# Storing h, q and V as high and low parts in a hybrid attention layer

## The chip, the cores and the metric

The kernel runs on one core of one Trainium2 chip. The metric is the device time of one execution in microseconds (us); a lower number is better. Each figure for a kernel as a whole is a median over several executions. Times inside the kernel come from one execution that the hardware profiler recorded.

The engines are named as in the profile: PE is the matmul engine (PEld its weight loads, which overlap its matmuls), DVE the vector engine, ACT the scalar engine, POOL the GpSimd engine, SP the engine that here issues every DMA transfer.

## The reference

One decoder layer over 2048 tokens of width 1024, in float32. Only the part that the change touches is shown in full.

```python
h = _rmsnorm(x, attn_pre_norm[l])
qkv = h @ w_qkv[l]                      # 1024 x 3072
dq, dk, dv, sq, sk, sv = jnp.split(qkv, QKV_SPLITS, axis=-1)
# group A: 4 heads, two softmax maps of 64 per head, values of 128
diff_o = _diff_attention(dq, dk, dv, lam, rel_bias)
diff_o = _rmsnorm(diff_o, diff_subln[l]) * (1.0 - lam_init)
# group B: 8 heads of 64, z = q k / 8, no softmax:
#   a = exp(log_sigmoid(z) + sum over later keys of log_sigmoid(-z)), strictly causal
sb_o = _rmsnorm(_stick_breaking_attention(sq, sk, sv), sb_norm[l])
mix = jnp.concatenate([diff_o, sb_o], axis=-1) @ w_o[l]
x = x + _rmsnorm(mix, attn_post_norm[l])
h = _rmsnorm(x, ffn_pre_norm[l])
u = _causal_depthwise_conv(h @ w_up[l], conv_w[l], conv_b[l])
gate, val = jnp.split(u, 2, axis=-1)
y = (jax.nn.gelu(gate, approximate=True) * val) @ w_down[l]
x = x + _rmsnorm(y, ffn_post_norm[l])
```

## The kernel before

**High and low parts.** A matmul takes its operands in the type float32r, which keeps fewer bits than float32. Each float32 operand is therefore split: the high part is the value rounded to float32r (a cast), the low part the value minus the high part (a subtraction). A product is then three matmuls, high by high, high by low and low by high. The helper `split` (lines 454 to 462) makes both parts from a raw float32 piece in SBUF: the cast on DVE (line 457) or ACT (458), the subtraction on POOL (459) or DVE (461).

**Order of the work.** Nothing is issued where it is written. Every step is recorded as an operation with a cost in ns per engine that could do it, and `Plan.run` (line 180) then simulates the engines by these costs and issues each operation on the engine that is free first, the nominally earliest ready one first. All engines run their lists in order, so the costs (`c_act`, `c_dvp`, `c_scan` and others, lines 43 to 68) decide on which engine a copy lands and in which order. SP has one list for all transfers.

**Stages.** (1) `prep` makes h for 256 tokens at a time (8 token tiles): rows of x are normed, transposed on PE into PSUM tiles `t`, and leave PSUM three times: high part to `hT` on ACT (line 575), low part to `hT` on DVE (577), and a raw float32 copy to `ring_a` on ACT (581), from which `store_h` (588) writes h to the DRAM tensor `hd`. (2) The projection to q, k and V runs in five passes over the 8 token tiles, because only three units of 256 columns of w_qkv fit on chip at once. Pass 0 uses the `hT` that `prep` made; in passes 1 to 4 `load_h` (line 528) loads the raw h of a tile from `hd` into the ring `ring_w` and splits it into `hT`. That is 32 tiles of two halves, each half 128x1024 elements.

(3) `evac` (line 619) takes a finished product out of PSUM (`g`) through a staging tile `st` (two buffers) to DRAM. q leaves raw, scaled on ACT (line 634), and is stored by line 643 to `qd`; V leaves raw (466 or 467) and is stored by 629 to `vd`; k is already split here, high part on ACT or DVE, low part on DVE (638), both stored by 646 to `kd`.

(4) 64 attention units (g, s), g one of 8 head pairs, s one of 8 blocks of 256 queries. `load_q` (698) and `load_kv` (678) fetch their operands. k goes straight to its tile `k`. q goes raw to `ring_w` and is split into the tile `q` (two buffers); V goes raw to `ring_w` and is split into `v` (five buffers). Units with g below 4 are differential attention (`diff_front`, `diff_back`), the others stick-breaking (`sb_stream`). In a stick-breaking unit each chunk of logits goes through two sigmoids on ACT (978, 980), a running product along the keys on DVE (986, called the scan below), a multiplication on POOL (991), transposes on PE (729) to `t`, a split of these into `thi` (ACT 466 or DVE 467) and `tlo` (DVE 743), and the products with V on PE (1009). At a unit's end `fin_sb` norms the result (DVE 813, 816, 825, POOL 815). The projection's passes 1 to 4 are merged into the attention units, spread evenly.

(5) The output projection, merged with the last units, and (6) the FFN, neither of which the change touches.

The rings `ring_w` (8192 columns) and `ring_a` (4096) hold pieces of any length in order of use; the attention's rows of logits live there too.

Of the kernel before, what the change touches and what calls it, by code (L numbers as in the profile page):

```python
# [15 lines left out]
F32 = mybir.dt.float32  # L16
# [8 lines left out]
P = 128  # L25
# [16 lines left out]
# Costs in ns, by which the order of issue is planned.  # L42
# [16 lines left out]
def c_scan(n):  # L59
    return 130 + 1.6 * n  # L60
# [59 lines left out]
class Ring(Tag):  # L120
    """Pieces of any length, one after the other, round and round."""
# [145 lines left out]
def layer_kernel(  # L267
# [149 lines left out]
    def setup_bias():  # L417
# [11 lines left out]
        v4 = lambda: br.t.rearrange("p (h c) -> p h c", h=4)  # noqa: E731  # L429
# [25 lines left out]
    def split(raw, hi, lo, n, deps, bufs, lead):  # L455
        """hi + lo = raw exactly"""
# [7 lines left out]
    def copy(dst, src, n, deps, bufs, what=None):  # L464
        """out of PSUM"""
# [3 lines left out]
    class Unit:  # L469
# [55 lines left out]
    hcur, hdep, hraw, hstore, xin = {}, {}, {}, {}, {}  # L525
    qstore, kstore, vstore = defaultdict(list), defaultdict(list), defaultdict(list)

    def load_h(p, i):
        hcur[p, i] = [buf("hT"), buf("hT")]
        hdep[p, i] = []  # L530
        for c in range(2):
            h, raw = hcur[p, i][c], buf("w", 1024)
            rv = lambda raw=raw: raw.t.rearrange("p (k n) -> p k n", k=4)  # noqa: E731
            o = load(rv, hd[i][:, c * 4:(c + 1) * 4, :], 1 << 19, (raw,), (hstore[i, c],), what="hload")
            hdep[p, i] += [split(rv, lambda h=h: h.t[:, 0], lambda h=h: h.t[:, 1], 1024, (o,), (raw, h), 0.0)] * 4
# [9 lines left out]
    def prep(i, gdep):  # L545
        """x rows -> normed, transposed, split"""
# [13 lines left out]
        hraw[i] = [(buf("a", 1024), []) for _ in range(2)]  # L560
        for k2 in range(4):
# [875 lines left out]
```

## Time and profile before

| | |
|---|---|
| median of 3 runs | 3197.41 us (3193.2 to 3203.99) |
| span of the profiled execution | 3198.2 us |
| PE busy | 3010.5 us, 94% |
| PEld busy | 2627.1 us, 82% |
| DVE busy | 2370.5 us, 74% |
| ACT busy | 1550.6 us, 48% |
| POOL busy | 1141.6 us, 36% |
| DMA | 353.25 MB moved, mean 110 GB/s |

The profiled execution's span differs from the median by 0.8 us, so the span is taken as its whole time. The busy shares are means over stages that have different limits: from about 740 us on the stick-breaking heads run, from about 1460 us their end and the output projection, from about 1760 us the FFN. A row of the profile names the line, the engine, the operation, the tile written and the tiles read, the shape, the number of such instructions, and then the time.

### The profile page before, as it was taken

Reading aid. Unit: us, or ns where it says so; the run is one execution under the profiler, and the core shown is the slowest. Engines: PE = TensorE matmul, PEld = TensorE weight load, DVE = VectorE, ACT = ScalarE, POOL = GpSimd, SP = SyncE. Lnnn points to the kernel's source line nnn. Section 1 sums busy time; section 2 is a strip of 40 time slices with the busy share of each in tenths; the row PEclk is TensorE's granted clock in tenths of the full one; section 3 lists DMA queues with packets and bytes.
Section 4 is the critical chain, followed back from the end, with each engine's and each line's share of the span. In section 5 each row is a group of like instructions: output and inputs, shape, how many; then the busy total and the mean of one; then the engine's idle time right before and its main releaser. Section 6 shows DMA issues by size and latency. Waiting matters only on the chain. (4 is left out here: it accounts for less than half of the span.)

```text
span 3198.2 us, 48493 instructions
## 1 busy us (share of the span) xinstructions
PE 3010.5 (94%) x17352; PEld 2627.1 (82%) x17352; DVE 2370.5 (74%) x4310; ACT 1550.6 (48%) x3098; POOL 1141.6 (36%) x1135
## 2 busy tenths in 40 slices
PE   7999999999888788878999999999999999999998
PEld 7999999989777687777877888888888888888887
DVE  4588979898999999998865676367753877367742
ACT  5555655656666666665654343223332333223421
POOL 1131223224777777775522211023310333023310
PEclk9999999999999999998999999999999999999999
DMA  6553334423322123142245333343334433343342
GB/s 219 177 151 97 96 95 128 118 67 100 107 73 60 52 83 102 58 109 88 99 154 175 115 106 98 120 148 96 97 121 123 123 103 93 125 139 99 94 131 79
DMA packets 371669, 353.25 MB, mean 110 GB/s; under 512 B 20096, under 2 KB 311780, under 8 KB 371428
## 3 DMA queue, kind: packets, MB, share of 16 engines
q1 hardware_dynamic: 371428, 350.16, 36.3%
q8 instruction: 136, 2.23, 0.3%
q14 instruction: 105, 0.86, 0.1%
HBM read 274.58 MB, written 75.50 MB: 109 GB/s over the span
## 5 line engine op out<-in xcount | busy, mean ns | idle before, releaser
L1235 PE MATMUL pu<-fh,fhi 128*128 128x512 f32 x2816 | 868.2, 390 | 0.2 <-ACT fu L1243 0.2
L1235 PEld LDWEIGHTS pu<-fh,fhi 128*128 128x128 f32 x2816 | 529.1, 188 | 110.6 <-ACT fu L1243 0.6
L461 DVE TENSOR_TENSOR flo<-fraw,fhi 128x1024 fp32r<-128x1024 f32 x186 | 232.9, 1254 | 487.0 <-ACT fhi L458 486.9
L1235 PE MATMUL pu<-fh,flo 128*128 128x512 f32 x1408 | 548.5, 390 | 0.0
L991 POOL TENSOR_TENSOR ring_w<-ring_w,ring_a 128x512 f32<-128x512 f32 (+2 forms) x320 | 407.8, 1289 | 203.1 <-DVE ring_a L986 144.6
L458 ACT CAST fhi<-fraw 128x1024 fp32r<-128x1024 f32 x253 | 265.6, 1051 | 397.0 <-PE py L1320 220.9
L613 PE MATMUL g<-hT,big 128*128 128x256 f32 x3072 | 451.6, 288 | 3.6 <-POOL big L459 1.9
L986 DVE TENSOR_TENSOR_SCAN ring_a<-ring_a 128x513 f32<-128x513 f32 (+2 forms) x320 | 433.5, 1379 | 3.7 <-ACT ring_a L978 3.3
L1320 PE MATMUL py<-fhi,gt 128*128 128x512 f32 x1408 | 435.7, 390 | 0.0
L613 PEld LDWEIGHTS g<-hT,big 128*128 128x128 f32 x3072 | 407.3, 192 | 12.8 <-POOL big L459 2.3
L711 PE MATMUL z<-k,q 128*128 128x512 f32 (+3 forms) x1280 | 364.4, 379 | 12.6 <-ACT ring_a L978 6.1
L466 ACT CAST thi<-t 128x512 fp32r<-128x512 f32 (+2 forms) x461 | 217.8, 492 | 212.5 <-PE t L729 187.9
L459 POOL TENSOR_TENSOR flo<-fraw,fhi 128x1024 fp32r<-128x1024 f32 x78 | 195.8, 2511 | 339.2 <-DVE fhi L457 171.2
L1320 PEld LDWEIGHTS py<-fhi,gt 128*128 128x128 f32 x1408 | 264.3, 188 | 60.5
L1235 PEld LDWEIGHTS pu<-fh,flo 128*128 128x128 f32 x1408 | 264.6, 188 | 55.3
L743 DVE TENSOR_TENSOR tlo<-t,thi 128x512 fp32r<-128x512 f32 (+2 forms) x528 | 281.4, 557 | 34.0 <-ACT thi L466 25.6
L729 PE MATMUL t<-ident,ring_w 128*128 128x128 f32 x1632 | 262.3, 282 | 40.5 <-DVE tlo L743 22.1
L1259 POOL TENSOR_TENSOR gt<-fy,gt 128x512 fp32r<-128x512 f32 x88 | 118.4, 1346 | 493.9 <-ACT gt L1258 477.1
L1320 PE MATMUL py<-flo,gt 128*128 128x512 f32 x704 | 277.4, 394 | 0.0
L729 PEld LDWEIGHTS t<-ident,ring_w 128*128 128x128 f32 x1632 | 194.2, 144 | 61.5 <-issue 16.3
L1248 DVE SCALAR_TENSOR_TENSOR fy<-fu,cw,fy 128x512 f32<-128x512 f32 x176 | 239.8, 1363 | 6.2
L610 PE MATMUL g<-big,hT 128*128 128x256 f32 x1536 | 226.5, 286 | 0.0
(170 smaller groups left out, 5009.5 us busy)
## 6 DMA issues: line engine op xcount, KB each, us to landing
fraw<-in_w_up_dram SPq DMA_DIRECT2D x176, 512.0 KB, 3.8
fraw<-in_w_down_dram SPq DMA_DIRECT2D x88, 512.0 KB, 3.7
ring_w<-hd SPq DMA_DIRECT2D x64, 512.0 KB, 5.0
kd<-st SPq DMA_DIRECT2D x128, 128.0 KB, 2.5
k<-kd SPq DMA_DIRECT2D x32, 512.0 KB, 4.8
ring_w<-qd SPq DMA_DIRECT2D x128, 128.0 KB, 3.7
ring_w<-in_x_dram SPq DMA_DIRECT2D x16, 512.0 KB, 4.5
hd<-ring_a SPq DMA_DIRECT2D x16, 512.0 KB, 2.8
```

The source lines that it names most:

```text
L458: "ACT", c_act(n) + 42, lambda: nc.scalar.copy(hi(), raw()))
L461: "DVE", c_dvs(n), lambda: nc.vector.tensor_tensor(lo(), raw(), f32(hi()), ALU.subtract))
L610: nc.tensor.matmul(ps.t[:, cs], hk[:, b, c * P:(c + 1) * P], wv[:, a, k, :], start=first, stop=last)
L613: nc.tensor.matmul(ps.t[:, cs], wv[:, a, k, c * P:(c + 1) * P], hk[:, b, :], start=first, stop=last)
L711: nc.tensor.matmul(ps.t[:, 0:w], q.t[:, m, l, jj * P:(jj + 1) * P], kt.t[:, m, 0:w], start=(l == 0), stop=(l == 1 and not masked))
L729: nc.tensor.transpose(ps.t[:, cc * P:(cc + 1) * P], rows[jj].t[:, (k + kk) * P:(k + kk + 1) * P], ident)
L743: ol = op("DVE", c_dvp(n), lambda sl=sl: nc.vector.tensor_tensor(lo.t[:, sl], ps.t[:, sl], f32(hi.t[:, sl]), ALU.subtract), (oh,), (ps, hi ...
L986: nc.vector.tensor_tensor_scan(gr, gr, gr, 1.0 if cb is None else cb[0].t[:, 0:1], ALU.mult, ALU.bypass)
L991: rdeps.append(op("POOL", c_pool(w), lambda be=be, gm=gm, w=w: nc.gpsimd.tensor_tensor(be.t, be.t, gm.t[:, 1:w + 1], ALU.mult), (o1, o2), ...
L1235: nc.tensor.matmul(ps.t, w3(w)[:, k, :], h.t[:, a, k, :], start=(k == 0 and i == 0), stop=(k == KD - 1 and i == 2))
L1248: nc.vector.scalar_tensor_tensor(y.t, u.t[:, 1:TT + 1], cw[:, 1, f:f + 1], y.t, ALU.mult, ALU.add)
L1320: nc.tensor.matmul(ps.t, gt.t[:, a, j * P:(j + 1) * P], wt.t[:, ms], start=(m == 0 and i == 0), stop=(m == NFT - 1 and i == 2))
```

## The change

h, q and V are split once, where they are made, the two parts are stored side by side in DRAM, and the loads write both parts directly into the tiles that the matmuls read. `hd`, `qd` and `vd` have twice the bytes. The raw copy of h in `ring_a` and the raw pieces in `ring_w` are gone, and with them 64 splits of h, 64 of q and 32 of V. In `evac` each q and each V gets a low part on DVE (64 and 64 instructions of 128x256). The planner's cost of a scan, `c_scan`, is another one. Comments are dropped; the lines of after.py are therefore up to 9 lower.

```diff
 def c_scan(n):
-    return 130 + 1.6 * n
+    return 130 + 2.083 * n
...
-    qd = [dram.tile([64, 2, S], F32, name=f"qd{g}") for g in range(8)]
+    qd = [dram.tile([64, 2, 2, S], F32, name=f"qd{g}") for g in range(8)]
...
-    vd = [dram.tile([S, 256], F32, name=f"vd{u}") for u in range(4)]
-    hd = [dram.tile([P, KD, 256], F32, name=f"hd{i}") for i in range(8)]
+    vd = [dram.tile([2, 4, P, 4, 256], F32, name=f"vd{u}") for u in range(4)]
+    hd = [dram.tile([2, P, KD * 256], F32, name=f"hd{i}") for i in range(8)]
...
     def load_h(p, i):
...
-            h, raw = hcur[p, i][c], buf("w", 1024)
-            rv = lambda raw=raw: raw.t.rearrange("p (k n) -> p k n", k=4)
-            o = load(rv, hd[i][:, c * 4:(c + 1) * 4, :], 1 << 19, (raw,), (hstore[i, c],), what="hload")
-            hdep[p, i] += [split(rv, lambda h=h: h.t[:, 0], lambda h=h: h.t[:, 1], 1024, (o,), (raw, h), 0.0)] * 4
+            h = hcur[p, i][c]
+            o = load(lambda h=h: f32(h.t).rearrange("p a k n -> p (a k n)"), hd[i][c], 1 << 20, (h,), (hstore[i, c],),
+                     what="hload")
+            hdep[p, i] += [(o,)] * 4
...
     def prep(i, gdep):
...
-                raw, ops = hraw[i][k // 4]
-                ops.append(op("ACT", c_act(256) + 95, lambda raw=raw, pk=pk, k=k: nc.scalar.activation(
-                    raw.t[:, k % 4 * 256:(k % 4 + 1) * 256], pk(), AF.Identity, scale=g_pre[:, k:k + 1]), (o, gdep),
-                    (ps, raw)))
-        store_h(i)
...
+        for c in range(2):
+            ops = [o for pair in hdep[0, i][4 * c:4 * c + 4] for o in pair]
+            hstore[i, c] = op(SPE, 0, lambda c=c: nc.sync.dma_start(
+                hd[i][c], f32(h[c].t).rearrange("p a k n -> p (a k n)")), ops, (h[c],), 0, 1 << 20, "hstore")
...
         def evac(c):
...
             if is_v:
-                o = copy(lambda: tf()[:, 0:256], pc, 256, (st["last"],), (ps, t))
...
+                o1 = copy(lambda: t5(0), p4, 256, (st["last"],), (ps, t))
+                o = op("DVE", c_dvp(256), lambda: nc.vector.tensor_tensor(t5(1), p4(), f32(t5(0)), ALU.subtract),
+                       (o1,), (ps, t))
+                vstore[spec, i].append(op(SPE, 0, lambda: nc.sync.dma_start(
+                    vd[spec][:, r0 // 4, :, r0 % 4, :].rearrange("g p c -> p g c"),
+                    tf().rearrange("p (g c) -> p g c", g=2)), (o,), (t,), 0, 1 << 18, "vstore"))
...
             if kind == "q":
-                o = op("ACT", c_act(256), lambda: nc.scalar.activation(tf()[:, 0:256], pc(), AF.Copy, scale=0.125),
-                       (st["last"],), (ps, t))
+                o1 = op("ACT", c_act(256), lambda: nc.scalar.activation(t.t[:, 0:256], pc(), AF.Copy, scale=0.125),
+                        (st["last"],), (ps, t))
+                o = op("DVE", c_dvp(256), lambda: nc.vector.scalar_tensor_tensor(
+                    t.t[:, 256:512], pc(), 0.125, f32(t.t[:, 0:256]), ALU.mult, ALU.subtract), (o1,), (ps, t))
...
     def load_kv(g, c):
...
-        raw = buf("w", 512)
...
-            vs = split(r5, lambda: v5()[:, :, :, 0, :], lambda: v5()[:, :, :, 1, :], 512, (o,), (raw, v), 0.0)
-        kv[g, c] = (kt, v, ok, vs)
+        ov = load(lambda: f32(v.t), vd[g // 2][g % 2, c], 1 << 19, (v,),
+                  [o for i in tiles for o in vstore[g // 2, i]], what="vload")
+        kv[g, c] = (kt, v, ok, (ov,))
 
     def load_q(g, s):
-        q, raw = buf("q"), buf("w", 512)
+        q = buf("q")
...
-        qt[g, s] = q, split(rv, lambda: q.t[:, :, 0, :], lambda: q.t[:, :, 1, :], 512, ls, (raw, q), 0.0)
+        qt[g, s] = q, [load(lambda r=r: f32(q.t[r * 64:(r + 1) * 64]), qd[g][:, :, :, s * 256:(s + 1) * 256], 1 << 18,
+                            (q,), qstore[g, s], what="qload") for r in range(2)]
```

What this makes of the engines' lists is seen at two places. The first is DVE in the stick-breaking stage, at the same scans of the same unit. `hT`, `q` and `v` are matmul tiles, `ring_a` the rows of the scan, `tlo` the low part of transposed rows, `st` the staging tile of `evac`, `os`, `sq`, `sm` and `mix` tiles of `fin_sb`. Before:

```order
L743 TENSOR_TENSOR tlo_186<-t_145,thi_184 128x512
L986 SCALAR_TENSOR_TENSOR ring_a<-ring_a 128x513
L461 TENSOR_TENSOR hT_161<-ring_w,hT_161 128x1024
L816 TENSOR_REDUCE sm_204<-sq_191 128x4
L743 TENSOR_TENSOR tlo_187<-t_146,thi_185 128x512
L382 TENSOR_SCALAR sm_203<-sm_204 128x4
L986 SCALAR_TENSOR_TENSOR ring_a<-ring_a 128x513
```

And now:

```order
L734 TENSOR_TENSOR tlo_186<-t_145,thi_184 128x512
L807 TENSOR_REDUCE sm_200<-sq_191 128x4
L624 TENSOR_TENSOR st_164<-g_148,st_164 128x4x64
L382 TENSOR_SCALAR sm_205<-sm_200 128x4
L624 TENSOR_TENSOR st_165<-g_148,st_165 128x4x64
L734 TENSOR_TENSOR tlo_187<-t_146,thi_185 128x512
L977 SCALAR_TENSOR_TENSOR ring_a<-ring_a 128x513
```

The 128x1024 subtraction for `hT` out of the ring is gone from between the scans; two subtractions of 128x256 elements that read PSUM (`g`) stand there for V.

The second place is SP at the start of pass 4, with the semaphores that each transfer waits for in brackets (DMAHW is an earlier transfer). Before:

```order
L646 DMA kd_73<-st_165 64x2x256 [waits DMAHW2_49]
L377 DMA ring_w<-hd_80 128x1024 [waits DMAHW3_49]
L377 DMA ring_w<-hd_80 128x1024 [waits DMAHW4_49,Pool_49]
L775 DMA mixd_88<-mo_188 128x256 [waits DMAHW5_49,Activation_49]
L629 DMA vd_78<-st_164 128x256 [waits DMAHW6_49,Activation_49]
L629 DMA vd_78<-st_165 128x256 [waits DMAHW7_49,Activation_49]
L377 DMA ring_w<-qd_64 64x2x256 [waits DMAHW0_49,PE_49]
```

And now:

```order
L647 DMA kd_73<-st_165 64x2x256 [waits DMAHW2_49]
L766 DMA mixd_88<-mo_188 128x256 [waits DMAHW3_49,Activation_49]
L377 DMA hT_158<-hd_80 128x2048 [waits DMAHW4_49,PE_49]
L377 DMA hT_159<-hd_80 128x2048 [waits DMAHW5_49,PE_49]
L377 DMA q_179<-qd_64 64x4x256 [waits DMAHW6_49,PE_49]
L377 DMA q_179<-qd_64 64x4x256 [waits DMAHW7_49]
L626 DMA vd_78<-st_164 128x2x256 [waits DMAHW0_49,DVE_49]
```

The loads of h and q now wait for PE to release `hT` and `q` themselves, and the store of V, which waits for DVE instead of ACT, stands behind them.

## Rows read from the trace of the kernel before

**Rows 1.** The page: busy tenths in 40 slices of 80 us each.

```profile
PE   7999999999888788878999999999999999999998
DVE  4588979898999999998865676367753877367742
DMA  6553334423322123142245333343334433343342
```

**Rows 2.** Windows by stage: length, busy us (count) per engine, clock, DMA share, GB/s.

```profile
0.00:160.00 160.00, 142.55 (x1146) 138.80 (x1147) 79.12 (x222) 92.00 (x232) 23.41 (x31) 1.00 0.64 198
160.00:740.00 580.00, 560.83 (x4237) 532.36 (x4235) 508.06 (x1594) 336.51 (x706) 151.16 (x109) 0.99 0.38 107
740.00:1460.00 720.00, 597.92 (x4250) 544.69 (x4249) 693.73 (x911) 477.06 (x1061) 528.60 (x657) 0.96 0.29 83
1460.00:1760.00 300.00, 280.07 (x1438) 232.02 (x1437) 214.50 (x334) 162.66 (x403) 112.78 (x152) 0.97 0.40 130
1760.00:3198.20 1438.20, 1429.17 (x6290) 1179.21 (x6288) 875.05 (x1254) 482.39 (x697) 325.62 (x188) 1.00 0.36 112
```

**Rows 3.** Waits of PE, 740 to 1460 us: total us, times, longest.

```profile
PE t L772 <- DVE tlo L743: 34.5, 19, 3.4
PE o L1009 <- DVE tlo L743: 23.5, 26, 2.3
```

**Rows 4.** DVE by shape, 740 to 1460 us: count, busy us, mean ns, idle before.

```profile
L986 DVE TENSOR_TENSOR_SCAN ring_a<-ring_a 128x513 f32<-128x513 f32 x186 | 285.0, 1552 | 0.1
...
L825 DVE SCALAR_TENSOR_TENSOR mix<-os,sm,sbn 128x64 f32<-128x64 f32 x108 | 66.6, 675 | 1.8 <-POOL sm L384 0.9 <-POOL ring_a L976 0.9
...
L461 DVE TENSOR_TENSOR hT<-ring_w,hT 128x1024 fp32r<-128x1024 f32 x15 | 25.0, 1664 | 0.0
...
L461 DVE TENSOR_TENSOR v<-ring_w,v 128x512 fp32r<-128x512 f32 x8 | 11.7, 1466 | 0.0
...
L461 DVE TENSOR_TENSOR q<-ring_w,q 128x512 fp32r<-128x512 f32 x12 | 10.1, 841 | 0.0
L467 DVE CAST thi<-t 128x512 fp32r<-128x512 f32 x14 | 9.5, 680 | 4.1 <-PE t L729 3.9 <-PE o L1009 0.2
L638 DVE TENSOR_TENSOR st<-g,st 128x256 fp32r<-128x256 f32 x22 | 8.7, 408 | 0.8 <-ACT st L466 0.8
L457 DVE CAST hT<-ring_w 128x1024 fp32r<-128x1024 f32 x4 | 5.1, 1274 | 0.0
```

**Rows 5.** One line or tile: count, ns min/median/max, first and last start.

```profile
L825 DVE SCALAR_TENSOR_TENSOR mix<-os,sm,sbn x108: 254/449/2373, 780.9 to 1439.7; 128x64 f32<-128x64 f32 x108
...
L638 DVE TENSOR_TENSOR st<-g,st x64: 392/415/426, 39.9 to 1431.9; 128x256 fp32r<-128x256 f32 x64
...
L575 ACT ACTIVATE hT<-t,g_pre x64: 462/476/557, 13.8 to 156.4; 128x256 fp32r<-128x256 f32 x64
```

**Rows 6.** POOL by shape, 740 to 1460 us.

```profile
L991 POOL TENSOR_TENSOR ring_w<-ring_w,ring_a 128x512 f32<-128x512 f32 x185 | 265.4, 1446 | 110.5 <-DVE ring_a L986 77.5 <-ACT thi L466 9.9 <-PE t L729 7.1
L459 POOL TENSOR_TENSOR hT<-ring_w,hT 128x1024 fp32r<-128x1024 f32 x19 | 51.4, 2707 | 4.1 <-DVE hT L457 4.1
...
L459 POOL TENSOR_TENSOR q<-ring_w,q 128x512 fp32r<-128x512 f32 x16 | 24.4, 1523 | 1.6 <-ACT q L458 1.6
```

**Rows 7.** Timeline, instructions merged: start us, us, what, count.

```profile
1066.96 4.97 DVE L986 TENSOR_TENSOR_SCAN ring_a<-ring_a 128x385 f32<-128x385 f32 x2
...
1067.82 3.02 POOL L459 TENSOR_TENSOR hT<-ring_w,hT 128x1024 fp32r<-128x1024 f32 x1
...
1099.53 1.25 DVE L986 TENSOR_TENSOR_SCAN ring_a<-ring_a 128x513 f32<-128x513 f32 x1
```

**Rows 8.** DMA issues: count, KB each, median us to landing.

```profile
ring_w<-hd SPq DMA_DIRECT2D x64, 512.0 KB, 5.0
...
ring_w<-qd SPq DMA_DIRECT2D x128, 128.0 KB, 3.7
hd<-ring_a SPq DMA_DIRECT2D x16, 512.0 KB, 2.8
```

More of the change, by code (lines that the diff above doesn't have):

```diff
@@ L524, in layer_kernel @@
     ]
-    hcur, hdep, hraw, hstore, xin = {}, {}, {}, {}, {}
+    hcur, hdep, hstore, xin = {}, {}, {}, {}
     qstore, kstore, vstore = defaultdict(list), defaultdict(list), defaultdict(list)
@@ L559, in prep @@
         hdep[0, i] = []
-        hraw[i] = [(buf("a", 1024), []) for _ in range(2)]
         for k2 in range(4):
@@ L579, in prep @@
                 hdep[0, i].append((o1, o2))
-                raw, ops = hraw[i][k // 4]
-                ops.append(op("ACT", c_act(256) + 95, lambda raw=raw, pk=pk, k=k: nc.scalar.activation(
-                    raw.t[:, k % 4 * 256:(k % 4 + 1) * 256], pk(), AF.Identity, scale=g_pre[:, k:k + 1]), (o, gdep),
-                    (ps, raw)))
-        store_h(i)
-    def store_h(i):
-        for c, (raw, ops) in enumerate(hraw[i]):
-            hstore[i, c] = op(SPE, 0, lambda raw=raw, c=c: nc.sync.dma_start(
-                hd[i][:, c * 4:(c + 1) * 4, :], raw.t.rearrange("p (k n) -> p k n", k=4)), ops, (raw,), 0, 1 << 19,
-                "hstore")
+        for c in range(2):
+            ops = [o for pair in hdep[0, i][4 * c:4 * c + 4] for o in pair]
+            hstore[i, c] = op(SPE, 0, lambda c=c: nc.sync.dma_start(
+                hd[i][c], f32(h[c].t).rearrange("p a k n -> p (a k n)")), ops, (h[c],), 0, 1 << 20, "hstore")
     def unit_steps(p, i, unit, spec):
@@ L626, in evac @@
             if is_v:
-                o = copy(lambda: tf()[:, 0:256], pc, 256, (st["last"],), (ps, t))
-                r0 = i * 256 + c * P
-                vstore[spec, i].append(op(SPE, 0, lambda: nc.sync.dma_start(vd[spec][r0:r0 + P], tf()[:, 0:256]),
-                                          (o,), (t,), 0, 1 << 17, "vstore"))
+                r0 = i * 2 + c
+                nh, dh = (1, P) if spec < 2 else (2, 64)
+                t5 = lambda l: t.t.rearrange("p (g h l d) -> p g h l d", g=2, h=nh, l=2)[:, :, :, l, :]
+                p4 = lambda: pc().rearrange("p (g h d) -> p g h d", g=2, h=nh)
+                o1 = copy(lambda: t5(0), p4, 256, (st["last"],), (ps, t))
[4 more added lines that the diff above has]
+                    tf().rearrange("p (g c) -> p g c", g=2)), (o,), (t,), 0, 1 << 18, "vstore"))
                 return
@@ L641, in evac @@
                 ms = slice(m * 64, (m + 1) * 64)
+                tl = lambda ms=ms: tf()[ms].rearrange("p (l s) -> p l s", l=2)
                 if kind == "q":
-                    qstore[g, i].append(op(SPE, 0, lambda m=m, ms=ms: nc.sync.dma_start(
-                        qd[g][:, m, cs], tf()[ms, 0:256]), (o,), (t,), 0, 1 << 16, "qstore"))
-                else:
-                    kstore[g, i].append(op(SPE, 0, lambda m=m, ms=ms: nc.sync.dma_start(
-                        kd[g].rearrange("(l d) m s -> d l m s", l=2)[:, :, m, cs],
-                        tf()[ms].rearrange("p (l s) -> p l s", l=2)), (o,), (t,), 0, 1 << 17, "kstore"))
+                    qstore[g, i].append(op(SPE, 0, lambda m=m, tl=tl: nc.sync.dma_start(
+                        qd[g][:, m, :, cs], tl()), (o,), (t,), 0, 1 << 17, "qstore"))
+                else:
+                    kstore[g, i].append(op(SPE, 0, lambda m=m, tl=tl: nc.sync.dma_start(
+                        kd[g].rearrange("(l d) m s -> d l m s", l=2)[:, :, m, cs], tl()), (o,), (t,), 0, 1 << 17,
+                        "kstore"))
         for c in range(2):
@@ L684, in load_kv @@
                   what="kload")
-        raw = buf("w", 512)
-        rv = lambda: raw.t.rearrange("p (b n) -> p b n", b=4)
-        o = load(rv, vd[g // 2][cs].rearrange("(b p) c -> p b c", p=P)[:, :, g % 2 * P:(g % 2 + 1) * P], 1 << 18,
-                 (raw,), [o for i in tiles for o in vstore[g // 2, i]], what="vload")
-        if g < 4:
-            vs = split(rv, lambda: v.t[:, :, 0:P], lambda: v.t[:, :, P:256], 512, (o,), (raw, v), 0.0)
-        else:
-            v5 = lambda: v.t.rearrange("p b (h l d) -> p b h l d", h=2, l=2)
-            r5 = lambda: raw.t.rearrange("p (b h d) -> p b h d", b=4, h=2)
-            vs = split(r5, lambda: v5()[:, :, :, 0, :], lambda: v5()[:, :, :, 1, :], 512, (o,), (raw, v), 0.0)
-        kv[g, c] = (kt, v, ok, vs)
+        ov = load(lambda: f32(v.t), vd[g // 2][g % 2, c], 1 << 19, (v,),
+                  [o for i in tiles for o in vstore[g // 2, i]], what="vload")
+        kv[g, c] = (kt, v, ok, (ov,))
     def load_q(g, s):
-        q, raw = buf("q"), buf("w", 512)
+        q = buf("q")
         assert qstore[g, s]
-        rv = lambda: raw.t.rearrange("p (m s) -> p m s", m=2)
-        ls = [load(lambda r=r: rv()[r * 64:(r + 1) * 64], qd[g][:, :, s * 256:(s + 1) * 256], 1 << 17, (raw,),
-                   qstore[g, s], what="qload") for r in range(2)]
-        qt[g, s] = q, split(rv, lambda: q.t[:, :, 0, :], lambda: q.t[:, :, 1, :], 512, ls, (raw, q), 0.0)
+        qt[g, s] = q, [load(lambda r=r: f32(q.t[r * 64:(r + 1) * 64]), qd[g][:, :, :, s * 256:(s + 1) * 256], 1 << 18,
+                            (q,), qstore[g, s], what="qload") for r in range(2)]
     def zchunk(g, s, m, jj, c, w, masked, lead):
```

## The prediction

> **What bounds the kernel now.** First the slices of the page, then the windows by stage, then what PE waits for, then the groups of the busiest engine in the stage where PE waits. The slices show PE at 9 nearly throughout, except at the start and between slices 10 and 20, where DVE stands at 9 [rows 1]. The windows put numbers to it [rows 2]. PE idles 17.4 us of 160 in the first stage, 19.2 of 580 in the differential heads, 122.1 of 720 in the stick-breaking heads, 19.9 of 300 in their end with the output projection, 9.0 of 1438.2 in the FFN. In the stick-breaking stage DVE is busy 693.7 of 720 us (96%), and the two largest waits of PE are both for `tlo`, which DVE makes: 34.5 and 23.5 us [rows 3]. So PE bounds everything but one stage, and there DVE does. Time taken off DVE between 740 and 1460 us is worth its length, as long as PE stays behind it. Elsewhere the change can win little more than part of PE's idle time.
>
> The time before is the profiled span, 3198.2 us; the median is 0.8 us lower, which is inside what can be told. A measurement of this kernel tells some 0.3% (9.6 us) from no change.
>
> **What the change takes off DVE in the stick-breaking stage.** Of the splits that go away, DVE did 15 subtractions for `hT` (25.0 us), 8 for `v` (11.7), 12 for `q` (10.1) and 4 casts for `hT` (5.1): 51.9 us [rows 4].
>
> **What it adds there.** In the new order of DVE 42 of the 128 new low parts (22 of V, 20 of q) stand among the 274 scans that ran in this stage. Their nearest row is the low part of k: the same shape, one input in PSUM, 408 ns [rows 4]. 42 by 0.408 is 17.1 us. That row never goes above 426 ns in 64 [rows 5], whereas the removed 128x1024 subtraction averages 1664 ns. I take 408 for all.
>
> **What the planner moves.** ACT loses 64 raw copies of h and most casts of the splits, and the dearer scan makes DVE look fuller to the planner. In the same stretch of DVE's list stand 11 fewer casts of `thi` of 512 columns (680 ns each [rows 4]: 7.5 us), 6 narrower ones (0.3 to 0.4 us: 2), 8 fewer copies of 256 columns (as the 408 ns row: 3.3), 3 fewer of 512 columns (2.0) and 5 fewer subtractions for the weights (as the `q` row, 841 ns: 4.2). That is 19 us. They go to ACT, which is busy 477 of 720 us and itself gets lighter, and to POOL, 529 of 720 [rows 2]. So the direct sum on DVE is 51.9 - 17.1 + 19 = 54 us. If none of the moved copies counted it would be 35.
>
> **What goes with POOL.** DVE's instructions that read only SBUF vary widely. A scan over 513 columns takes 1.25 us at 1099.53 and 1552 ns in the mean of 186; the norm of line 825 has a minimum of 254, a median of 449 and a mean of 675 ns [rows 4, 5, 7]. The cause shows at 1066.96: two scans together last 4.97 us while a POOL subtraction for `hT` runs 3.02 us from 1067.82 [rows 7]; the mean of 186 longer scans would make it 3.1. So a DVE instruction over SBUF alone is held while POOL works. The surplus of these two groups is 186 by 0.302 plus 108 by 0.421, 102 us. POOL's removed work here is 19 subtractions for `hT` (51.4 us), 16 for `q` (24.4) and a few for `v`, beside 185 multiplications of 512 columns (265.4) and others, of 528.6 us in all [rows 2, 6]. By busy time `hT` and `q` hold 75.8/528.6 = 14% of the surplus, 15 us. But a long POOL instruction is both hit more often and holds longer, so weights of count times length squared are nearer: 19 by 2.707 squared and 16 by 1.523 squared are 139 and 37, against 387 for the multiplications, 31%, or 32 us. I take 25, nearer to the upper end because the row at 1067.82 shows a nearly whole hold.
>
> The Trainium skill says in "SBUF — State Buffer", section "Who interferes with whom", that a DVE instruction with two SBUF inputs and a GpSimd instruction that reads SBUF exclude each other, the later one blocking fully until the first is done. By that rule the hold is the rest of the POOL instruction, and the term is the 32 us; without any such rule it would be 0. The row of 3.02 us speaks for the rule.
>
> DVE's relief is then 54 + 25 = 79 us, with 35 and 86 as ends.
>
> **What is late next there.** 720 - 79 is 641 us, in which PE's 597.9 us of work are 93% [rows 2]. In the differential stage, where PE is the bound, it reaches 560.8 of 580, 96.7%; at that rate the stage can't go under 618 us. DVE would be at (693.7 - 79)/641 = 96%. So DVE still ends last, but two engines with in-order lists are both nearly full, and part of the relief becomes idle time of the other. I take 7 off: 72 us saved.
>
> The Trainium skill says in "Perfetto Trace Analysis", section "Identifying the Most-Contended Engine", that matmul busy time is a bad measure of PE's headroom and the weight loads' share a better one. Weight loads are busy 544.7 of 720 us here [rows 2]. By that measure PE is not near its bound, nothing is taken off, and the next rival is what follows.
>
> **The first stage.** 64 activations of `ring_a` leave ACT, at about the 476 ns of their twin for `hT` [rows 5], 30 us; ACT is busy 92 of 160 us and PE's idle time there is mostly the start, so I take nothing. The transfers grow: 8 MB more for h, 2 for q, 2 for V. At 198 GB/s and a share of 0.64 [rows 2] the 31.7 MB of this stage become 43.7 and the share 0.88, an estimate by proportion. That is hidden while the share stays under 1; if peaks expose a quarter of the 12 MB at 198/0.64 = 309 GB/s, it costs 10 us. I take 0, with -5 and +10 as ends.
>
> **Other stages.** In the differential heads DVE gets the larger part of the new low parts (86, at 408 ns: 35 us) and loses its part of the splits and their holds; it has 72 us of slack and PE's idle time is 19.2. I take 3 us saved, from 10 saved to 12 lost. In the end of the stick-breaking heads 46 scans are left and 7 subtractions move to POOL: 2 saved. The FFN is not touched: 0.
>
> **Loads.** Before, raw pieces came to `ring_w` ahead of time, and only a split waited for the tile. Now the transfer itself waits for the last matmul that read `hT` or `q`, on SP, and stores queue behind it. A load of 512 KB lands in 5.0 us, one of 128 KB in 3.7 [rows 8]. By that slope 1 MB takes some 7, two halves issued together about 10. There are two sets of `hT`, so a load has a whole token tile as cover: in the stick-breaking stage 34 halves, 17 tiles, were split in 720 us [rows 4, 6], 42 us a tile. For q the cover is the unit in between, shorter than the load only where s is 0. The cast and subtraction that stood there before took over 2 us as well. I take 0.
>
> **Sum.** 3198.2 - 72 - 3 - 2 = **3121 us**.
>
> **The rivals.** (1) *PE closes its gaps.* `tlo` reaches PE earlier everywhere, relief is at its upper end of 86 us, and the granted clock, 0.96 in this stage against 0.99 before it [rows 2], comes back: 598 by 0.03 is 18 us of PE's time. Then 3198.2 - 86 - 5 - 18 = about 3090. For it: PE's waits are nearly all on DVE. Against: no stage of this kernel before the FFN runs without 3% of idle time.
>
> (2) *The hold stays.* POOL's multiplications follow the scans closely; with fewer subtractions between them they run right behind each scan and hold the next, and the copies that ACT took come late. Then only 35 us are relieved and 28 to 30 gained: 3169. For it: the multiplications have by far the largest weight in the surplus.
>
> (3) *It does nothing.* The freed time of DVE is filled with waits of the same size, since order and buffers are the planner's: 3198. Against it: DVE's idle time in this stage has hardly a wait for another engine in its rows; it is simply full.
>
> (4) *Late loads, slower.* 32 tiles of `hT` are loaded after the projection's passes have begun. If SP's list runs behind, each load comes after PE has already drained the tile, with the stores of `st` queued behind it, and `evac` stalls too. At 4 us exposed of the 10 for each of 32 tiles that is 128 us against 77 gained: about 3249. It is slower than before from 2.4 us exposed per tile on. Against it: a tile of pass 1 has 144 matmuls at 132 ns (560.83 us for 4237 [rows 2]), 19 us even without any attention beside it, and later tiles are spread over 42 us.
>
> **How the numbers follow.** Forecast 0.53, rival 1 0.18, rival 2 0.17, rival 3 0.05, rival 4 0.07. The forecast's own range is 3095 to 3150; to hold 8 in 10 the range takes most of rivals 1 and 2: 3080 to 3172. Faster by over 0.3% are the forecast and rivals 1 and 2: 0.88. Within it rival 3: 0.05. Slower rival 4: 0.07.
>
> **What would show it.** In the changed kernel's profile the stretch from the first scan to the end of the projection should be some 70 us shorter, with all else in place. The scans of 513 columns should average about 1.45 us instead of 1552 ns. POOL's busy time should fall by about 170 us, ACT's by over 100, the DMA volume should rise by about 80 MB. PE's waits for `tlo` should shrink. If the scans' mean stays, the term of POOL was wrong; if PE waits for `hT` or `q`, the loads were; if the stage is no shorter although DVE is at 85%, the order of the lists is the bound.

## The result and the profile after

The changed kernel takes 3089.17 us in the median (3087.65 to 3094.23, 4 runs) against 3198.56 us before: a ratio of 0.9662, 95% interval 0.9647 to 0.9677, or 109 us less. 77 us less were forecast. The sign, the stage and the mechanism came out as forecast; the gain is 32 us larger than its sum. The profiled span is 3092.5 us, 105.7 us under the one before, and the ledger below is made against that.

First the slices of the page and the windows by stage (length; busy us and count of PE, PEld, DVE, ACT, POOL; clock, DMA share, GB/s). The cuts lie at the same work as in [rows 2]: the first scan, the 274th scan, and a place in the FFN. The FFN itself begins earlier than said above: its first matmul starts at 1689.6 us before and at 1583.8 now.

```profile
PE   7999999999999999889999999999999999999998
DVE  4658878897999999998754864387744776277742
DMA  8776656655634366533363333443344333343332
```

```profile
0.00:160.00 160.00, 134.29 (x1000) 126.57 (x1001) 90.89 (x275) 68.42 (x160) 17.81 (x27) 0.97 0.80 254
160.00:738.00 578.00, 572.36 (x4393) 547.44 (x4392) 479.15 (x1605) 286.88 (x639) 53.03 (x60) 1.00 0.61 176
738.00:1359.00 621.00, 570.40 (x4245) 524.35 (x4244) 594.82 (x872) 443.47 (x1019) 433.37 (x615) 0.99 0.52 153
1359.00:1660.00 301.00, 283.99 (x1456) 236.56 (x1457) 215.97 (x331) 163.20 (x406) 122.67 (x159) 0.97 0.41 135
1660.00:3092.50 1432.50, 1423.44 (x6265) 1175.49 (x6263) 871.20 (x1246) 480.92 (x693) 324.68 (x187) 1.00 0.37 111
```

Read against [rows 1, 2]: the dip of PE between slices 10 and 20 has nearly gone, and the third window is 621 us where it was 720. Taken to the hundredth, from the start of the first scan to that of the 274th it was 716.8 us and is 620.6: 96.2 of the 105.7 us. The first scan starts 4.0 us earlier, the end of the stick-breaking heads, up to the FFN's first matmul, is 5.6 us shorter, and the FFN takes 1508.6 us in both, counted from its first matmul.

PE's waits in this stretch (us in total, times, longest), against [rows 3], are still for `tlo`, but shorter:

```profile
PE t L720 <- DVE tlo L734: 15.4, 16, 2.7
PE t L763 <- DVE tlo L734: 13.8, 14, 2.0
PE z L702 <- ACT ring_a L969: 7.0, 11, 1.0
```

No wait of PE for a load of `hT`, `q` or `v` stands in the whole trace. The groups of DVE and of POOL there (count, busy us, mean ns), against [rows 4, 6]:

```profile
L977 DVE TENSOR_TENSOR_SCAN ring_a<-ring_a 128x513 f32<-128x513 f32 x186 | 273.3, 1487 | 0.9 <-ACT ring_a L969 0.9
L734 DVE TENSOR_TENSOR tlo<-t,thi 128x512 fp32r<-128x512 f32 x189 | 123.6, 671 | 8.5 <-ACT thi L466 5.8 <-PE o L1000 1.2 <-PE o L911 0.9
L816 DVE SCALAR_TENSOR_TENSOR mix<-os,sm,sbn 128x64 f32<-128x64 f32 x108 | 46.7, 491 | 3.2 <-POOL ring_a L967 2.3 <-POOL sm L384 0.8
...
L977 DVE TENSOR_TENSOR_SCAN ring_a<-ring_a 128x129 f32<-128x129 f32 x30 | 19.0, 635 | 1.6 <-ACT ring_a L969 1.6
...
L624 DVE TENSOR_TENSOR st<-g,st 128x256 fp32r<-128x256 f32 x22 | 8.5, 408 | 0.0
L634 DVE SCALAR_TENSOR_TENSOR st<-g,st 128x256 fp32r<-128x256 f32 x20 | 8.0, 402 | 0.0
...
L467 DVE CAST thi<-t 128x512 fp32r<-128x512 f32 x3 | 2.0, 671 | 0.0
```

```profile
L982 POOL TENSOR_TENSOR ring_w<-ring_w,ring_a 128x512 f32<-128x512 f32 x185 | 248.6, 1353 | 122.7 <-DVE ring_a L977 77.9 <-PE t L720 14.1 <-ACT thi L466 10.0
...
L459 POOL TENSOR_TENSOR big<-raw,big 128x512 fp32r<-128x512 f32 x17 | 27.9, 1642 | 4.0 <-DVE big L457 3.0 <-PE z L702 1.0
```

The 42 new low parts cost 16.5 us, 402 and 408 ns each. The scans of 513 columns fell from 1552 to 1487 ns, the norm's instruction of 64 columns from 675 to 491 ns, though neither was touched. The loads (count, KB each, median us to landing), against [rows 8]:

```profile
hT<-hd SPq DMA_DIRECT2D x64, 1024.0 KB, 7.0
...
q<-qd SPq DMA_DIRECT2D x128, 256.0 KB, 4.3
hd<-hT SPq DMA_DIRECT2D x16, 1024.0 KB, 5.4
```

### The profile page after: what moved, and what is told of

Its sections match the earlier page's. It is cut to its first block, busy times and chain, and to the rows that moved or that the text cites. A ratio compares the mean times of both kernels' runs of the same rounds, so it can differ in the third digit from the quotient of the medians.

```text
span 3092.5 us, 48117 instructions
## 1 busy us (share of the span) xinstructions
PE 2984.5 (97%) x17352; PEld 2610.4 (84%) x17352; DVE 2252.0 (73%) x4327; ACT 1442.9 (47%) x2913; POOL 951.6 (31%) x1047
## 5 line engine op out<-in xcount | busy, mean ns | idle before, releaser
L982 POOL TENSOR_TENSOR ring_w<-ring_w,ring_a 128x512 f32<-128x512 f32 (+2 forms) x320 | 387.9, 1224 | 220.3 <-DVE ring_a L977 121.1
L977 DVE TENSOR_TENSOR_SCAN ring_a<-ring_a 128x513 f32<-128x513 f32 (+2 forms) x320 | 412.8, 1316 | 6.1 <-ACT ring_a L969 6.1
L720 PE MATMUL t<-ident,ring_w 128*128 128x128 f32 x1632 | 253.2, 276 | 22.4 <-DVE tlo L734 18.5
L384 POOL TENSOR_TENSOR sm<-sm,neghalf 128x2 f32<-128x2 f32 (+1 forms) x72 | 76.8, 1067 | 536.5 <-DVE sm L382 534.7
```

Source lines behind the costliest of these rows:

```text
L720: nc.tensor.transpose(ps.t[:, cc * P:(cc + 1) * P], rows[jj].t[:, (k + kk) * P:(k + kk + 1) * P], ident)
L977: nc.vector.tensor_tensor_scan(gr, gr, gr, 1.0 if cb is None else cb[0].t[:, 0:1], ALU.mult, ALU.bypass)
L982: rdeps.append(op("POOL", c_pool(w), lambda be=be, gm=gm, w=w: nc.gpsimd.tensor_tensor(be.t, be.t, gm.t[:, 1:w + 1], ALU.mult), (o1, o2), ...
```

## The experiments

**Theory.** The stretch of the scans is bound by DVE, and its gain is DVE's relief: the splits that DVE itself no longer does, the copies that the planner moved off it, and the time for which its SBUF instructions were held by POOL's subtractions. **Rivals.** The hold plays no part and the gain comes from the moved copies; or the new scan cost in the plan makes the gain, and the storage none; or the order of the lists does, which no sum over instructions tells.

The table has, for every kernel, the median, the ratio to before with its interval, and then from its profiled execution the stretch from the first scan to the 274th: length, DVE busy, the difference (DVE idle), PE busy, all in us, and the mean ns of the scans of 513 columns (186) and of the norm's instruction (108). The runs of before beside the experiments had medians of 3196.1 to 3197.0 us; a gain against before is taken from those.

| kernel | median | ratio (95%) | length | DVE | DVE idle | PE | scan | norm |
|---|---|---|---|---|---|---|---|---|
| before | 3198.56 | 1 | 716.8 | 691.1 | 25.7 | 594.7 | 1552 | 675 |
| after | 3089.17 | 0.9662 (0.9647-0.9677) | 620.6 | 594.4 | 26.2 | 570.2 | 1487 | 491 |
| a_raw_h | 3162.96 | 0.9886 (0.9864-0.9908) | 680.5 | 650.5 | 30.0 | 588.7 | 1578 | 629 |
| a_raw_qv | 3144.5 | 0.9831 (0.9816-0.9846) | 661.6 | 621.7 | 39.9 | 583.0 | 1526 | 615 |
| a_low2 | 3114.1 | 0.9737 (0.9722-0.9751) | 628.8 | 598.3 | 30.5 | 572.1 | 1469 | 452 |
| a_poolwork | 3176.4 | 0.9933 (0.9918-0.9948) | 696.9 | 665.4 | 31.5 | 590.3 | 1568 | 826 |
| a_hold | 3167.74 | 0.9911 (0.9896-0.9926) | 693.1 | 657.5 | 35.6 | 589.0 | 1651 | 656 |
| a_oldscan | 3132.23 | 0.9795 (0.978-0.9811) | 648.2 | 603.4 | 44.8 | 575.7 | 1462 | 477 |
| b_newscan | 3184.18 | 0.9956 (0.9941-0.9971) | 704.4 | 673.2 | 31.2 | 602.2 | 1610 | 681 |
| a_old_hiact | 3118.91 | 0.9756 (0.9741-0.9771) | 634.4 | 591.9 | 42.5 | 567.4 | 1469 | 524 |
| a_scan20 | 3098.31 | 0.9692 (0.9678-0.9707) | 624.5 | 594.3 | 30.2 | 571.2 | 1467 | 495 |
| a_scan22 | 3089.54 | 0.9664 (0.9647-0.968) | 625.3 | 595.3 | 30.0 | 574.0 | 1496 | 522 |
| a_scan28 | 3103.09 | 0.9701 (0.9684-0.9717) | 636.4 | 581.3 | 55.1 | 581.1 | 1485 | 500 |
| a_st4 | 3091.22 | 0.9665 (0.965-0.9679) | 616.9 | 589.2 | 27.7 | 567.9 | 1466 | 490 |

**Storage or plan cost?** The change has two halves; each was undone alone. The changed kernel with the old cost of a scan:

```diff
-    return 130 + 2.083 * n
+    return 130 + 1.6 * n
```

> The changed kernel with the old planner cost of a scan (130 + 1.6 n). Theory (the gain is DVE's relief in the stick-breaking stage: splits gone, POOL's holds gone, copies moved): the order shows 13 casts of thi, 5 weight subtractions and some 9 other copies back on DVE in that stage, about 16 us, so some 3105 us, range 3095 to 3115. Rival A (the gain comes from the better plan that the new scan cost makes, not from the stored parts): most of the 109 us goes, 3150 us or more. Rival B (PE already bounds that stage after the change): within 5 us of 3089.

The kernel before with the new cost of a scan:

```diff
-    return 130 + 1.6 * n
+    return 130 + 2.083 * n
```

> The kernel before with only the new planner cost of a scan (130 + 2.083 n). Theory: some 17 us of copies and q subtractions leave DVE in the stick-breaking stage, but 7 of the q subtractions go to POOL, which then holds DVE a little more: 10 to 15 us faster, about 3186 us. Rival A (the plan is what gains): 3140 us or less.

The storage alone gives 65 us (3132), the cost alone 13 (3184), both together 109. So the storage is the larger half, the plan cost is not the gain by itself, and some 30 us appear only with both. The expectation for the first was a miss: 43 us lost instead of 16. Two readings of the runs bear on this; what makes the 30 us isn't shown. In a_oldscan DVE has only 9 us more work than in the changed kernel, but 18.6 us more idle time. In b_newscan the dearer scan pushes 7 splits of q off DVE, onto POOL, and the scans of 513 columns rise from 1552 to 1610 ns:

```profile
L986 DVE TENSOR_TENSOR_SCAN ring_a<-ring_a 128x513 f32<-128x513 f32 x186 | 295.5, 1610 | 3.8 <-ACT ring_a L978 3.8
...
L461 DVE TENSOR_TENSOR q<-ring_w,q 128x512 fp32r<-128x512 f32 x5 | 4.8, 963 | 0.0
```

```profile
L459 POOL TENSOR_TENSOR q<-ring_w,q 128x512 fp32r<-128x512 f32 x23 | 35.7, 1552 | 2.8 <-ACT q L458 2.7
```

So it may be that with the raw storage relief for DVE by way of POOL comes back as hold, while without it the planner has only copies left to move, which ACT takes. This isn't shown: the instructions that stay in DVE's list of b_newscan get only 5 to 8 us longer in sum, and the order of the list alone moves such a sum by up to 11 us (a_low2, below).

**One part at a time.** h stored raw as before, q and V stored split:

```diff
...
-            o = load(lambda h=h: f32(h.t).rearrange("p a k n -> p (a k n)"), hd[i][c], 1 << 20, (h,), (hstore[i, c],),
...
+            o = load(rv, hd[i][:, c * 4:(c + 1) * 4, :], 1 << 19, (raw,), (hstore[i, c],), what="hload")
+            hdep[p, i] += [split(rv, lambda h=h: h.t[:, 0], lambda h=h: h.t[:, 1], 1024, (o,), (raw, h), 0.0)] * 4
...
```

> The changed kernel with h stored raw again and split at every load (q and V stay as changed). Theory: in the stick-breaking stage DVE gets 9 subtractions of 128x1024, 5 casts and a few copies back, about 24 us, and POOL 25 subtractions of 2.6 us, whose holds give about 30 us back; the first stage wins back up to 8 us of PE idle time because the stores of h are half as large. About 3137 us, range 3120 to 3150. Rival C (the gain is mostly the direct work of DVE and holds are minor): about 3110 us.

q and V stored raw as before, h stored split:

```diff
...
-        q = buf("q")
+        q, raw = buf("q"), buf("w", 512)
...
+        qt[g, s] = q, split(rv, lambda: q.t[:, :, 0, :], lambda: q.t[:, :, 1, :], 512, ls, (raw, q), 0.0)
...
```

> The changed kernel with q and V stored raw again and split at every load (h stays as changed). Theory: DVE in the stick-breaking stage loses the 42 low parts (17 us) and gets about 22 us of splits and copies back; POOL gets about 34 subtractions of 1.4 us, holds of about 12 us: some 17 us slower, 3106 us, range 3095 to 3118. Rival C (holds are minor): about 3094 us.

Raw h costs 74 us, raw q and V 55, where 48 and 17 were expected: the order of the two is right, both sizes are too small. Together they would be 129, while undoing both at the new scan cost costs 95 (b_newscan). The split of h is the larger part, and q and V matter far more than their own 21.8 us on DVE [rows 4]: with q and V raw the scans go back to 1526 ns and the norm to 615, and DVE's idle time rises by 13.7 us.

Every new low part made twice:

```diff
                 o = op("DVE", c_dvp(256), lambda: nc.vector.tensor_tensor(t5(1), p4(), f32(t5(0)), ALU.subtract),
                        (o1,), (ps, t))
+                o = op("DVE", c_dvp(256), lambda: nc.vector.tensor_tensor(t5(1), p4(), f32(t5(0)), ALU.subtract),
+                       (o,), (ps, t))
...
```

> The changed kernel in which every low part of q and V in the evacuation is computed twice (the same values). 128 more DVE instructions of 0.41 us, 42 of them in the stick-breaking stage. Theory (DVE still bounds that stage, one us of DVE there is worth one us, and elsewhere it is hidden): 15 to 20 us slower, about 3106 us. Rival B (PE bounds that stage now): less than 6 us slower. Rival D (the evacuation chain itself is what is critical in the first passes): over 35 us slower, with PE idle in the first 160 us.

It costs 25 us (15 to 20 expected). The stretch of the scans is 8.2 us longer, not 17: the 42 repeated instructions average 402 to 410 ns again, but the held instructions got shorter at the same time (scan 1469, norm 452 ns). The first scan starts 13.8 us later; the 86 low parts of the earlier stage are not free when doubled, though DVE is idle there for 17% of the time.

**Is it the hold?** The changed kernel with a useless POOL subtraction of 128x1024 elements for each half of h in passes 2 to 4, once at its full planner cost:

```diff
             hdep[p, i] += [(o,)] * 4
+            if p >= 2:
+                junk = buf("w", 1024)
+                op("POOL", c_pool(1024), lambda h=h, junk=junk: nc.gpsimd.tensor_tensor(
+                    junk.t.rearrange("p (k n) -> p k n", k=4), f32(h.t[:, 0]), f32(h.t[:, 1]), ALU.subtract),
+                   (o,), (junk, h))
```

> The changed kernel with one extra POOL subtraction of 128x1024 (its result is used by nothing) after each load of half a tile of h in passes 2 to 4. It measures the hold by itself: no DVE work is added by hand, though the planner puts about 15 us of copies back on DVE in the stick-breaking stage. Theory (POOL's work holds DVE): 34 such instructions stand in that stage, holds of about 50 us, with the copies about 3150 us, range 3130 to 3165; the mean of the scans of 513 columns rises again from 1487 ns to 1550 or more. Rival C (POOL's work hardly holds DVE): the copies alone, about 3103 us, and the mean of the scans stays.

It costs 87 us, more than its range. But it isn't clean: the planner saw a fuller POOL and put 11 casts of `thi` and 7 wide subtractions back on DVE, some 14 us. The second has the same subtraction into a tile of its own and at a planner cost of 1 ns:

```diff
...
+                junk = buf("jk")
+                op("POOL", 1, lambda h=h, junk=junk: nc.gpsimd.tensor_tensor(
...
-    T["w"] = Ring(8 * 1024)
+    T["w"] = Ring(7 * 1024)
...
```

> The changed kernel, with one subtraction of 128x1024 elements on POOL added per half of h in passes 2 to 4 (48 in all, into a tile that nobody reads, so useless work); its cost in the plan is 1 ns, so that the planner moves next to nothing for it: DVE's list in the stick-breaking stage keeps the changed kernel's casts and copies (thi casts of 512 columns 3 against 3, wide low parts 5 against 7). It tells the hold by POOL apart from copies that move. Theory (a DVE instruction over SBUF alone waits while POOL works): some 35 of the subtractions fall into the stick-breaking stage; before the change 35 POOL subtractions for hT and q stood there, and their removal gave back an estimated 41 us on DVE, so scans of 513 columns rise from 1487 to about 1560 ns, the norm's 128x64 instruction from 491 to about 650 ns, DVE's busy time by 40 to 55 us, and the time to 3130 to 3150. Rival (POOL holds nothing, only the moved copies counted): scans and norm stay, time within 10 us of 3089. Rival of the prediction's busy-share weights: about 20 us, 3110.

Here DVE's list in the stretch is nearly that of the changed kernel. With the changed kernel's mean durations, the difference in counts is worth 0.8 us, downwards; all the rest of DVE's 63 us is longer instructions of the same kinds. DVE's and POOL's groups, 740 to 1437 us:

```profile
L982 DVE TENSOR_TENSOR_SCAN ring_a<-ring_a 128x513 f32<-128x513 f32 x186 | 303.9, 1651 | 0.3 <-ACT ring_a L974 0.3
L739 DVE TENSOR_TENSOR tlo<-t,thi 128x512 fp32r<-128x512 f32 x189 | 123.8, 669 | 9.6 <-ACT thi L466 5.9 <-PE o L1005 1.7 <-ACT st L466 1.1
L821 DVE SCALAR_TENSOR_TENSOR mix<-os,sm,sbn 128x64 f32<-128x64 f32 x108 | 64.6, 656 | 8.0 <-POOL sm L384 4.9 <-POOL ring_a L972 3.0
```

```profile
L538 POOL TENSOR_TENSOR jk<-hT 128x1024 f32<-128x1024 f32 x34 | 94.4, 2778 | 2.9 <-DMA hT<-hd 2.9
```

Scans and norm are dearer, and `tlo`, which reads PSUM and SBUF, is not (669 ns against 671). Single places show it. The timeline of POOL at three of the added subtractions, and below it that of DVE at the same times (start us, us):

```profile
749.27 2.40 POOL L538 TENSOR_TENSOR jk<-hT 128x1024 f32<-128x1024 f32 x1 [2.88 <-DMA hT<-hd]
...
792.22 2.38 POOL L538 TENSOR_TENSOR jk<-hT 128x1024 f32<-128x1024 f32 x1
...
1090.30 3.34 POOL L538 TENSOR_TENSOR jk<-hT 128x1024 f32<-128x1024 f32 x1
```

```profile
749.57 0.69 DVE L739 TENSOR_TENSOR tlo<-t,thi 128x512 fp32r<-128x512 f32 x1 [1.11 <-ACT thi L466]
...
792.28 2.98 DVE L821 SCALAR_TENSOR_TENSOR mix<-os,sm,sbn 128x64 f32<-128x64 f32 x4 [0.53 <-POOL sm L384]
...
1090.18 4.54 DVE L982 TENSOR_TENSOR_SCAN ring_a<-ring_a 128x513 f32<-128x513 f32 x2
```

At 749.57 `tlo` runs its 0.69 us in the middle of the subtraction. At 792.28 four norm instructions, some 0.25 us each when free [rows 5], take 2.98 us, because the first ends only with POOL's subtraction. At 1090.18 both are seen: POOL's subtraction, 2.4 us when free, takes 3.34, since a scan had begun 0.12 us before it and POOL waits for that; and the next scan waits for POOL, so that two scans of 1.25 us take 4.54. The hold is shown, in both directions. 94.4 us of POOL's subtractions lengthened DVE's instructions by 62 us, two thirds of their length. The time rose by 79 us, more than the 41 to 61 expected: besides DVE's 63 us, its idle time rose by 9.4 and the first scan came 5.8 us later. (The ring `ring_w` is 1024 columns shorter here; a_st4, with the same shorter ring, loses only 2 us.)

The other kernels in which POOL got such subtractions back, less what it gave up for `big`, give 32 us of longer DVE instructions for 66 (a_raw_h), 23 for 45 (a_raw_qv) and 57 for 76 (a_poolwork): half to three quarters. The order of the list alone moves such a sum too. In a_low2, with POOL's work unchanged, the instructions that both kernels have got 11 us shorter.

Not every DVE instruction over SBUF alone is held, as the prediction has it. In a_hold the reduction at a unit's end, which reads only `sq` in SBUF, runs its usual 0.42 us inside an added subtraction (POOL, then DVE):

```profile
1259.20 2.36 POOL L538 TENSOR_TENSOR jk<-hT 128x1024 f32<-128x1024 f32 x1
```

```profile
1259.27 0.42 DVE L812 TENSOR_REDUCE sm<-sq 128x4 f32<-128x256 f32 x1 [0.44 <-POOL sq L811]
```

None of the 28 of them in the stretch takes more than 0.42 us.

The Trainium skill has the rule in "SBUF — State Buffer", section "Who interferes with whom": a DVE instruction with two SBUF inputs and a GpSimd instruction that reads SBUF exclude each other, and whichever is later waits for all of the first. The trace agrees, for the scan and the norm's instruction as the later one (2.98 and 4.54 us) and for POOL as the later one (3.34 us); and `tlo`, with one input in PSUM, is not held (0.69 us), as the section says of instructions with at most one SBUF input outside the 2-port modes, which by the section `tensor_scalar` can enter.

**How does the plan cost work?** The old scan cost again, with all high parts of `thi` pinned to ACT:

```diff
-            oh = copy(lambda sl=sl: hi.t[:, sl], lambda sl=sl: ps.t[:, sl], n, (o,), (ps, hi), "hi")
+            oh = op("ACT", c_act(n), lambda sl=sl: nc.scalar.copy(hi.t[:, sl], ps.t[:, sl]), (o,), (ps, hi), what="hi")
```

> The changed kernel with the old cost of a scan (1.6 ns a column), as in the run that took 3132 us, but with every high-part cast of thi pinned to ACT. In that run DVE had 16 casts of thi of 512 columns in the stick-breaking stage, here none. Theory 1 (the dearer scan works by pushing casts off DVE): without the 16 casts the time falls most of the way back, 3095 to 3110. Theory 2 (it works by the order of the lists): about 3130 again.

13 of the 43 us come back, neither of the two times expected. DVE's work falls by 11.5 us, below that of the changed kernel, but its idle time stays at 42.5 us. So the casts are about a third of what the old cost costs, and the rest is idle time of DVE and what lies around the stretch. Which rows of the order make it wasn't found.

Three other costs, 2.0, 2.2 and 2.6 ns a column:

```diff
-    return 130 + 2.083 * n
+    return 130 + 2.0 * n
```

> The changed kernel with a scan's cost of 2.0 ns a column in the plan in place of 2.083. Theory 1 (the number matters by which copies it moves: 5 thi casts of 512 columns on DVE against 3, 7 copies of the norm's result against 6, 11 wide low parts against 7): 3 to 6 us slower, 3092 to 3096. Theory 2 (any other number gives another order of the lists, and with it a time that differs by some 15 us without a reason that can be read off): anywhere from 3080 to 3110.

> The changed kernel with a scan's cost of 2.2 ns a column in the plan in place of 2.083. Theory 1 (the number matters by which copies it moves: 4 thi casts of 512 columns on DVE against 3, 1 copy of the norm's result against 6, 5 wide low parts against 7): some 3 us faster, 3084 to 3088. Theory 2 (any other number gives another order of the lists, and with it a time that differs by some 15 us without a reason that can be read off): anywhere from 3080 to 3110.

> The changed kernel with a planner cost of a scan of 130 + 2.6 n, 1461 ns for 512 columns, close to the measured mean of 1487 ns. Theory: a few more copies move from DVE to ACT in the stick-breaking stage, 3 to 10 us faster, about 3083 us. Rival B (PE bounds that stage): no change.

From 1.6 to 2.6 the times are 3132, 3098, 3089, 3090 and 3103 us: the ends are dear and the middle is flat. Both a_scan20 and a_scan22 lie some 2 us above the range that the moved copies would give, and all three new times lie in the range of theory 2, so five costs don't tell a curve from scatter. At the dear end the expected gain turned into a loss of 14 us, and DVE's waits tell why: it has 13 us less work and 29 us more idle time, most of it for ACT. First the waits of DVE in the stretch of a_scan28 (us in total, times, longest), then the first of them in the changed kernel:

```profile
DVE tlo L734 <- ACT thi L466: 28.4, 34, 2.3
DVE os L804 <- ACT os L466: 7.1, 10, 1.3
```

```profile
DVE tlo L734 <- ACT thi L466: 6.8, 10, 1.6
```

A free scan of 513 columns takes 1.25 us [rows 7]. The costs give it 0.95, 1.16, 1.20, 1.26 and 1.46 us; the best two lie nearest to the free duration, though these runs don't show that this is the reason.

**The first stage.** PE's idle time in the first 160 us went from 17.4 to 25.7 us. Four staging tiles `st` instead of two test whether the longer chain of `evac` is the cause:

```diff
-    for name, n in (("hT", 4), ("big", 3), ("raw", 2), ("st", 2), ("k", 5), ("v", 5), ("q", 2),
+    for name, n in (("hT", 4), ("big", 3), ("raw", 2), ("st", 4), ("k", 5), ("v", 5), ("q", 2),
...
```

> The changed kernel with four staging tiles st instead of two (ring_w 1024 columns shorter). PE idles 25.7 us in the first 160 us of the changed kernel, 17.4 before. If the longer chain through st (high part, low part, a store that is twice as large) causes it, PE's idle time there falls to 19 us or less and the kernel gains 4 to 8 us: about 3083 us. If the DMA engines are simply full there (share 0.80), nothing changes: 3089 us within 4.

Nothing changes (3091 us; 24.3 us of PE idle time). The staging tiles are not the cause. With h raw that idle time is 21.3 us, with q and V raw 24.0, at DMA shares of 0.72 and 0.70 against 0.80; this fits the transfers but doesn't show it, and the cause stays open.

## Why the prediction was nearly right, and what it missed

**The bound: right.** DVE was busy 96.4% of the stretch and is 95.8% now; its idle time went from 25.7 to 26.2 us. The stretch got shorter by DVE's relief, 96.7 us, one for one.

**Removed and added work: right.** 51.9 us are gone; 42 low parts cost 16.5 us where 17.1 were forecast. The moved copies took some 21 us off DVE (19 forecast). With the 43 us below that is 99 us, 3 more than DVE's busy time fell, since the durations of successive DVE instructions overlap a little.

**The hold: the term that was mis-sized.** 25 us were taken; the instructions that stayed in DVE's list got 43 us shorter. Of that the scans of 513 columns give 11.7 and the norm 19.9 us [rows 4], together 31.6 of the 102 us of surplus, the 31% of the weights by count times length squared. That they agree so closely is luck: in a_low2 the same two groups move by 7.6 us with POOL's work unchanged. The step failed twice: it chose a value below its own better estimate, and it looked at two groups only. The scans of 129 columns, which in the kernel before took

```profile
L986 DVE TENSOR_TENSOR_SCAN ring_a<-ring_a 128x129 f32<-128x129 f32 x30 | 28.5, 949 | 0.0
```

went to 635 ns, another 9.5 us; the other groups give 2 us together. The rule behind the term, that all DVE instructions over SBUF alone are held, is too wide: the reduction isn't. a_hold measures the same coupling from the other side: two thirds of POOL's added time. Before, POOL's removed 85 us of subtractions, less 8 us that it gained for `big`, gave back 56%; the prediction had taken 33%.

**PE as the next bound: wrong.** Seven us were taken off because PE's 597.9 us of work would be 93% of the new length. But PE's busy time is not a constant: the stretch holds 4245 matmuls where it held 4250, and PE is busy 570.4 us instead of 597.9, while its granted clock went from 0.96 to 0.99 (of the two levels, 1.2 and 2.4 GHz, the lower was granted less often). Across the table PE's busy time falls with its idle time: 122.1 us of idle time and 594.7 busy before, 104.0 and 589.0 in a_hold, 50.4 and 570.2 after (b_newscan lies 14 us and a_scan28 9 us above that line, a_old_hiact 8 us below it). The friction turned out to be 0.5 us.

The Trainium skill, "Perfetto Trace Analysis", section "Identifying the Most-Contended Engine", holds that matmul busy time misjudges PE's headroom. The trace sides with it here: nothing had to be taken off, with weight loads at 524.4 of 621 us.

**Rival 1 gave the number, 3090, with half of its working.** The clock came back to 0.99 as it says, and PE's busy time fell by 27.5 us where it counted 18; what makes the rest isn't shown. But that was no gain of its own, since DVE ended the stretch; the gain was 96 us of DVE's relief where the rival had 86. Rival 2 fell with the scans' mean, rival 3 with the result, and rival 4 with PE's waits: 1 MB lands in 7.0 us, as estimated from the slope, and no load is waited for.

**Other stages: right in sum.** Before the first scan 4.0 us were saved (3 forecast), as the sum of a loss and a gain: PE's idle time rose by 8 us in the first 160 us, inside the bounds of -5 to +10, and fell by 13.6 after that, while PE was busy 1.4 us longer. The end gave 5.6 us instead of 2. All together: 4.0 + 96.2 + 5.6 = 105.8 us of span. That is 29 us more than the sum's 77: 18 by the hold, 6.5 by the friction, 4.6 by the other stages.

**What would show it.** The stretch is shorter and all else in place; POOL's busy time fell by 190 us (170 forecast), ACT's by 108 (over 100), the volume rose by 84 MB (80). Only the scans' mean of 1487 ns (1450 forecast) pointed to a smaller term than it was; the hold left the shorter instructions instead.

## What to carry to other kernels

Where DVE is the bound, POOL work is not free: each us of POOL's subtractions in SBUF cost DVE half to three quarters of a us here, so work taken off POOL counts. It counts in the scans, the norm's instruction and even one of 128x4 elements, but not in the reduction, nor in instructions with an input in PSUM. Don't cap a gain by an engine's busy time when that engine idles and its clock is below full: remeasure. In a planned kernel the costs belong to the change: storage and cost were worth 65 and 13 us alone and 109 together, and of five costs of one instruction the best two lay near its free duration; why the order of the lists costs what it does stays open.

## What was not expected of the hardware

The hold reaches instructions with almost no work in them. In a_hold an instruction of 128x4 elements takes 2.32 us behind the start of a POOL subtraction (DVE, then POOL):

```profile
1235.18 2.32 DVE L382 TENSOR_SCALAR sm<-sm 128x4 f32<-128x4 f32 x1
```

```profile
1234.13 3.30 POOL L538 TENSOR_TENSOR jk<-hT 128x1024 f32<-128x1024 f32 x1
```

This one reads a single tile, and is held nevertheless until POOL's end at 1237.43. In the mean of 27 it takes 545 ns there against 346 in the changed kernel.
